# Streaming encoder layer on one core: 32 of 44 k-tiles of the down projection with the activations standing, the weights streaming 512 columns, and the sum turned by VectorE's block transposes

## The chip, the cores and the metric

The program runs on one core of a Trainium2 chip. The metric is the device time of one execution in microseconds (us), as the median of several runs. Beside the runs stands one profiled execution, whose rows are read below.

## What is computed

The reference is one layer of an encoder for 384 tokens (256 of a prompt, 8x16 of samples): two kinds of attention, then a gated feed-forward block, then an added embedding. All tensors are fp32. The change touches the third line alone:

```python
h = h + rms_norm(mix, g_post_mix)
f = rms_norm(h, g_pre_ffn)                                # (384, 2048)
f = (jax.nn.silu(f @ w_gate) * (f @ w_up)) @ w_down      # 2048 -> 5632 -> 2048
h = h + rms_norm(f, g_post_ffn)
return h + jax.nn.sigmoid(h @ w_ple_gate) * (p @ w_ple)
```

## The kernel before

Each fp32 matmul is done as three matmuls of a reduced fp32 type: weights and activations are split into a high part (ScalarE copies with a cast: `wh`, `sh`, `fh`) and a low part (VectorE subtracts: `wl`, `sl`, `fl`), and high x high, low x high and high x low are added up in a PSUM bank.

Weights come from memory in tiles of 128x2048 (`raw`, three buffers, loads issued by SyncE). `weights` cuts a tile into two half tiles of 128x1024 and `split` makes a `wh` and a `wl` of each. `wh` and `wl` have three buffers each, so a new half tile can be split when TensorE has done its last matmul with the one three before it.

The feed-forward block goes by eleven units of 512 hidden features. `gate_up(u)` computes a unit with the activations standing (the loaded operand is a 128x128 piece of `fh` or `fl`) and the weights streaming 512 columns: three banks, one for each 128 tokens, for the gate, three for the up part. ScalarE takes the gate from its banks through a Silu into `z` (128 tokens x 512 features, three times), VectorE multiplies the up part into it. `z` has tokens on the partitions. 16 block transposes of VectorE (blocks of 32x32, each instruction 32x384) turn it into `zT` with features on the partitions, and `to_hl` splits that into `sh` and `sl`, two 128-feature pieces to a buffer, five buffers.

The down projection works on groups of such pieces, `FGROUPS = (8, 8, 8, 8, 8, 4)`, 44 k-tiles in all. A group runs as soon as its pieces and one more are there: after units 2, 4, 6, 8 and 10, and the last of 4 right behind. For each of 16 tiles of 128 output features the weights stand and the activations stream 384 columns (`mm3`), into a bank `dn`. In the first group ScalarE copies the bank to `acc`, later VectorE adds it. The sum has output features on the partitions, as the norm and the residual behind it (`residual`) want it.

A scheduler fixes the order of instructions on each engine when the program is built, by priorities (`tc.high_priority`: weight splits are pulled ahead) and by its own estimate of times. On the chip an engine runs its instructions in that order. PSUM banks come from two sets of four: `dn` and the gate part use one, the up part the other.

Of the kernel before, what the change touches and what calls it, by code (L numbers as in the profile page):

```python
# [15 lines left out]
P = 128  # L16
# [40 lines left out]
def layer(ctx: ExitStack, tc: tile.TileContext, I, O):  # L57
# [76 lines left out]
    def g(col, n=0):  # L134
        return gains[:, col + n:col + n + 1]
# [686 lines left out]
    acc = ffn.tile([P, NK, T], F32, name="acc")  # L822

    def sq_add(ss, src, first, eng=dve):
        if first:
# [7 lines left out]
    for n in range(NK):  # L833
        ps = bank("mix")[:, :T]
        gemm(ps, weights(I["wout"][n]), mix, NK)
        act.copy(out=acc[:, n], in_=ps)
        sq_add(sm, acc[:, n], n == 0)

    def residual(ss, gcol, split_hl):

        low = []
        for n in range(NK):
            with ExitStack() as order:
                if n >= LEAD:
# [43 lines left out]
    residual(sm, G_POST, lambda n: scaled_hl(f(n), hh[:, n], g(G_FPRE, n)))  # L888
    rf = ffn.tile([P, 3], F32, name="rf")

    def by_token(out, w, k):

        for c in range(3):
            ah, al = f(k, slice(c * P, (c + 1) * P))
            pe.matmul(out[c], lhsT=ah, rhs=w[0], start=k == 0, stop=False)  # L895
            pe.matmul(out[c], lhsT=ah, rhs=w[1], start=False, stop=False)  # L896
            pe.matmul(out[c], lhsT=al, rhs=w[0], start=False, stop=k == NK - 1)  # L897

    def first_unit():

        gu = [[bank("gu", tag) for _ in range(3)] for tag in "gs"]
        for c in range(NK // 2):
            raw = stream.tile([P, 2048], F32, name="raw", tag="raw")
            with tc.high_priority(offset=PRIO):
                if c == 0:
                    subs = []
                    for i in range(2):
                        piece = raw[:, i * 1024:(i + 1) * 1024]
                        sp.dma_start(out=piece, in_=I["wgu0"][c][:, i * 1024:(i + 1) * 1024])
                        subs += split(piece, 1024)  # L910
                else:
                    sp.dma_start(out=raw, in_=I["wgu0"][c])
                    subs = split(raw, 2048)
            for i in range(2):
                for n in range(2):
                    by_token(gu[n], at(subs[i], slice(None), slice(n * 512, n * 512 + 512)), 2 * c + i)
        return gu

    gu0 = first_unit()
# [9 lines left out]
    def gate_up(u):  # L929
# [21 lines left out]
        zT = ffn.tile([P, 4, T], F32, name="zT", tag="zT")  # L951
        src = z.rearrange("p c (n f) -> p c n f", n=4)
        dst = zT.rearrange("p n (c t) -> p c n t", c=3)
        for j in range(4):
            for i in range(4):
                rows, cols = slice(32 * i, 32 * i + 32), slice(32 * j, 32 * j + 32)
                dve.transpose(out=dst[cols, :, :, rows], in_=src[rows, :, :, cols])  # L957
# [11 lines left out]
    for gi, gn in enumerate(FGROUPS):  # L969
        while len(ready) < gn + (1 if todo else 0) and todo:  # L970
            ready += gate_up(todo.pop(0))
        for n in range(NK):
            if n % 2 == 0:
                per = gn * P
# [5 lines left out]
            if gi == 0:  # L980
                act.copy(out=acc[:, n], in_=ps)
                continue
            with tc.high_priority(offset=2 * PRIO if gi == len(FGROUPS) - 1 else 0):
                dve.tensor_tensor(out=acc[:, n], in0=acc[:, n], in1=ps, op=ALU.add)  # L984
                if gi == len(FGROUPS) - 1:
                    sq_add(sd, acc[:, n], n == 0)
        ready = ready[gn:]


    embedding(1, sd)  # L990
    h2 = Pair("h2")
# [141 lines left out]
```

## Time and profile before

| | us |
|---|---|
| median of 3 runs | 1902.37 (1901.04 to 1902.71) |
| the profiled execution | 1902.81 |
| its span, first to last instruction | 1901.0 |
| TensorE busy in the span | 1883.6 |
| VectorE busy | 974.7 |
| ScalarE busy | 690.2 |

The span is what the rows of the profile lie in; the profiled execution's time is 1.8 us longer. A busy time counts an engine as busy while any of its instructions has a row that runs. Matmul rows overlap, so the pace of TensorE is read from the starts of its rows. The granted TensorE clock is 0.998 of full speed over the span.

### The profile page before, as it was taken

Reading aid. Unit: us, or ns where it says so; the run is one execution under the profiler, and the core shown is the slowest. Engines: PE = TensorE matmul, PEld = TensorE weight load, DVE = VectorE, ACT = ScalarE, POOL = GpSimd, SP = SyncE. Lnnn points to the kernel's source line nnn. Section 1 sums busy time; section 2 is a strip of 40 time slices with the busy share of each in tenths; the row PEclk is TensorE's granted clock in tenths of the full one; section 3 lists DMA queues with packets and bytes.
Section 4 is the critical chain, followed back from the end, with each engine's and each line's share of the span. In section 5 each row is a group of like instructions: output and inputs, shape, how many; then the busy total and the mean of one; then the engine's idle time right before and its main releaser. Section 6 shows DMA issues by size and latency. Waiting matters only on the chain.

```text
span 1901.0 us, 24107 instructions
## 1 busy us (share of the span) xinstructions
PE 1883.6 (99%) x10026; PEld 1709.8 (90%) x10026; DVE 974.7 (51%) x1368; ACT 690.2 (36%) x1044; POOL 80.4 (4%) x122
## 2 busy tenths in 40 slices
PE   8999999999999999999999999999999999999998
PEld 8989998788999988889988998899888988899998
DVE  7445756754233395445334643554355435456753
ACT  4344545643233453333333222322232222325432
POOL 4000002411000000000000000000000000000010
PEclk9999999999999999999999999999999999999999
DMA  6333325635743333343333333333333333334351
GB/s 239 136 110 112 112 89 176 213 138 204 258 169 133 130 122 133 111 136 130 133 133 123 122 133 133 129 118 130 133 133 111 133 133 133 111 111 147 128 177 67
DMA packets 43311, 262.53 MB, mean 138 GB/s; under 512 B 5441, under 2 KB 6481, under 8 KB 17090
## 3 DMA queue, kind: packets, MB, share of 16 engines
q1 hardware_dynamic: 36018, 233.76, 35.7%
q0 software_dynamic: 7184, 27.23, 4.1%
q8 instruction: 78, 1.28, 0.3%
q14 instruction: 31, 0.25, 0.0%
HBM read 251.17 MB, written 8.75 MB: 137 GB/s over the span
## 4 chain that ended last, share of the span: by engine, by line
PE 78%; DVE 1%; ACT 0%; issue 0%; DVEq 0%; ACTq 0%
PE gu L896 12%; PE gu L897 12%; PE gu L895 12%; PE dn L101 6%; PE dn L100 6%; PE dn L99 6%; PE mix L101 2%; PE pg L99 2%; PE pg L101 2%; PE pg L100 2%; PE mix L99 2%; PE mix L100 2%; PE psc L774 2%; PE pol L800 2%; PE ps L704 0%; DVE zT L957 0%
## 5 line engine op out<-in xcount | busy, mean ns | idle before, releaser
L90 DVE TENSOR_TENSOR wl<-raw,wh 128x1024 fp32r<-128x1024 f32 (+2 forms) x426 | 512.0, 1203 | 652.5 <-ACT wh L89 651.5
L89 ACT CAST wh<-raw 128x1024 fp32r<-128x1024 f32 (+2 forms) x426 | 435.8, 1023 | 980.5 <-PE gu L897 448.8
L896 PE MATMUL gu<-wl,fh 128*128 128x512 f32 x1056 | 411.5, 390 | 0.1
L897 PE MATMUL gu<-wh,fl 128*128 128x512 f32 x1056 | 409.2, 389 | 0.0
L895 PE MATMUL gu<-wh,fh 128*128 128x512 f32 x1056 | 406.9, 389 | 0.1
L896 PEld LDWEIGHTS gu<-wl,fh 128*128 128x128 f32 x1056 | 198.2, 188 | 42.7 <-DVE wl L90 1.7
L895 PEld LDWEIGHTS gu<-wh,fh 128*128 128x128 f32 x1056 | 198.2, 188 | 41.3 <-ACT fh L113 0.4
L897 PEld LDWEIGHTS gu<-wh,fl 128*128 128x128 f32 x1056 | 198.2, 188 | 41.0
L99 PE MATMUL dn<-sh,wh 128*128 128x384 f32 x704 | 235.1, 334 | 0.0
L100 PE MATMUL dn<-sl,wh 128*128 128x384 f32 x704 | 235.1, 334 | 0.0
L101 PE MATMUL dn<-sh,wl 128*128 128x384 f32 x704 | 234.7, 335 | 0.0
L101 PEld LDWEIGHTS dn<-sh,wl 128*128 128x128 f32 x704 | 132.0, 188 | 1.3 <-DVE wl L90 1.3
L99 PEld LDWEIGHTS dn<-sh,wh 128*128 128x128 f32 x704 | 132.1, 188 | 0.2
L100 PEld LDWEIGHTS dn<-sl,wh 128*128 128x128 f32 x704 | 132.1, 188 | 0.2
L957 DVE STREAM_TRANSPOSE zT<-z 32x384 f32<-32x384 f32 x176 | 100.3, 570 | 2.8
L984 DVE TENSOR_TENSOR acc<-acc,dn 128x384 f32<-128x384 f32 x80 | 44.3, 553 | 99.2 <-PE dn L101 98.8
L99 PE MATMUL mix<-mixh,wh 128*128 128x384 f32 x256 | 85.6, 334 | 0.0
L101 PE MATMUL pg<-h2h,wl 128*128 128x384 f32 x256 | 85.5, 334 | 0.0
L100 PE MATMUL pg<-h2l,wh 128*128 128x384 f32 x256 | 85.5, 334 | 0.0
L100 PE MATMUL mix<-mixl,wh 128*128 128x384 f32 x256 | 85.5, 334 | 0.0
L101 PE MATMUL mix<-mixh,wl 128*128 128x384 f32 x256 | 85.5, 334 | 0.0
L99 PE MATMUL pg<-h2h,wh 128*128 128x384 f32 x256 | 82.6, 334 | 0.0
(358 smaller groups left out, 2417.9 us busy)
## 6 DMA issues: line engine op xcount, KB each, us to landing
raw<-in_wgu SPq DMA_DIRECT2D x87, 1024.0 KB, 4.8
raw<-in_wd SPq DMA_DIRECT2D x40, 1024.0 KB, 4.8
raw<-in_win SPq DMA_DIRECT2D x20, 1024.0 KB, 4.9
raw<-in_wout SPq DMA_DIRECT2D x16, 1024.0 KB, 4.8
raw<-in_wpg SPq DMA_DIRECT2D x10, 1024.0 KB, 4.8
raw<-in_wvg SPq DMA_DIRECT2D x8, 1024.0 KB, 4.9
keys<-in_ckT POOLq DMA_DIRECT2D x8, 1024.0 KB, 5.6
raw<-in_ck SPq DMA_DIRECT2D x8, 1024.0 KB, 5.0
```

Of the source, the lines that this page charges most:

```text
L89: act.copy(out=h[:, :n], in_=raw[:, c:c + n])
L90: dve.tensor_tensor(out=l[:, :n], in0=raw[:, c:c + n], in1=h.bitcast(F32)[:, :n], op=ALU.subtract)
L99: pe.matmul(out, lhsT=w[0], rhs=a[0], start=start, stop=False)
L100: pe.matmul(out, lhsT=w[0], rhs=a[1], start=False, stop=False)
L101: pe.matmul(out, lhsT=w[1], rhs=a[0], start=False, stop=stop)
L774: pe.matmul(ps[:, :HK], lhsT=q.rearrange("p h t -> p (h t)"), rhs=keys[:, j, i * HK:(i + 1) * HK], start=j == 0, stop=j == 4)
L800: pe.matmul(o, lhsT=vals[:, k, j * P:(j + 1) * P], rhs=pT[:, k], start=k == 0, stop=False)
L895: pe.matmul(out[c], lhsT=ah, rhs=w[0], start=k == 0, stop=False)
L896: pe.matmul(out[c], lhsT=ah, rhs=w[1], start=False, stop=False)
L897: pe.matmul(out[c], lhsT=al, rhs=w[0], start=False, stop=k == NK - 1)
L957: dve.transpose(out=dst[cols, :, :, rows], in_=src[rows, :, :, cols])
L984: dve.tensor_tensor(out=acc[:, n], in0=acc[:, n], in1=ps, op=ALU.add)
```

## The change

The first four groups (`TOKG = 4`, 32 k-tiles) now run like the gate and up parts: `chunk_by_token` lets the activations stand and streams the weights in pieces of 512 output features, from a new arrangement of the same weights (`wdt`). One chunk is 512 output features: three banks for the three token blocks, 8 k-tiles, 72 matmuls of 512 columns; a group has four chunks. The sum of these groups, in four tiles `chunk0` to `chunk3` of 128x1536, has tokens on the partitions. After the fourth group `turn` transposes each chunk into features on the partitions with 16 block transposes, 64 in all, one chunk into a fifth tile and each next one into the place of the last. The last two groups (8 and 4 k-tiles) run as before and add to the turned sum. The fifth tile takes the place of `zT`, and later `chunk3`.

`chunk_by_token` also serves `gate_up`. It works the last quarter of a bank set bank by bank (all four k-tiles of one token block, then of the next) where the loop was by k-tile before.

```diff
+    chunks = [ffn.tile([P, 4 * T], F32, name=f"chunk{i}") for i in range(5)]
+    by_tok = [x.rearrange("p (c f) -> p c f", c=3) for x in chunks]
+    by_feat = [x.rearrange("p (n t) -> p n t", n=4) for x in chunks]
...
+    def turn(dst, src):
+
+        src = src.rearrange("p c (n f) -> p c n f", n=4)
+        dst = dst.rearrange("p n (c t) -> p c n t", c=3)
+        for j in range(4):
+            for i in range(4):
+                rows, cols = slice(32 * i, 32 * i + 32), slice(32 * j, 32 * j + 32)
+                dve.transpose(out=dst[cols, :, :, rows], in_=src[rows, :, :, cols])
...
+    def chunk_by_token(banks, srcs, a, nk):
+
+        for q, src in enumerate(srcs):
+            subs = weights(src)
+            order = [(k, c) for k in range(4) for c in range(3)]
+            if q == nk // 4 - 1:
+                order = [(k, c) for c in range(3) for k in range(4)]
+            for k, c in order:
+                kk = 4 * q + k
+                ah, al = a(kk, slice(c * P, (c + 1) * P))
+                w = at(subs[k // 2], slice(None), slice((k % 2) * 512, (k % 2) * 512 + 512))
+                by_token(banks[c], ah, al, w, kk == 0, kk == nk - 1)
...
-                for q in range(4):
-                    subs = weights(I["wgu"][8 * (u - 1) + 4 * i + q])
-                    for k in range(4):
-                        by_token(banks, at(subs[k // 2], slice(None), slice((k % 2) * 512, (k % 2) * 512 + 512)), 4 * q + k)
+                at_u = 8 * (u - 1) + 4 * i
+                chunk_by_token(banks, [I["wgu"][at_u + q] for q in range(4)], f, NK)
...
+        if gi < TOKG:
+            for n in range(4):
+                banks = [bank("dn") for _ in range(3)]
+                at_n = 8 * gi + 2 * n
+                chunk_by_token(banks, [I["wdt"][at_n + q] for q in range(2)],
+                               lambda k, t: (ready[k][0][:, t], ready[k][1][:, t]), 8)
+                for c in range(3):
+                    if gi == 0:
+                        act.copy(out=by_tok[n][:, c], in_=banks[c])
+                    else:
+                        dve.tensor_tensor(out=by_tok[n][:, c], in0=by_tok[n][:, c], in1=banks[c], op=ALU.add)
+            ready = ready[gn:]
+            if gi == TOKG - 1:
+
+                acc = []
+                for n in range(4):
+                    turn(by_feat[n - 1 if n else 4], by_tok[n])
+                    acc += [by_feat[n - 1 if n else 4][:, i] for i in range(4)]
+            continue
```

The order of VectorE's queue shows what moves. The first place is the border between the fourth group of the down projection and unit 9. Before, VectorE adds a bank (`acc`) and splits a half tile (`wl`) in turn, then splits for unit 9 (from `wl_10073` on):

```order
L984 TENSOR_TENSOR acc_4419<-acc_4419,dn_9932 128x384
L90 TENSOR_TENSOR wl_10027<-raw_10024,wh_10026 128x1024
L984 TENSOR_TENSOR acc_4419<-acc_4419,dn_9968 128x384
L90 TENSOR_TENSOR wl_10031<-raw_10024,wh_10030 128x1024
L109 TENSOR_TENSOR sl_9519<-zT_9495,sh_9518 128x384 x2
L984 TENSOR_TENSOR acc_4419<-acc_4419,dn_9994 128x384
L90 TENSOR_TENSOR wl_10073<-raw_10070,wh_10072 128x1024
L90 TENSOR_TENSOR wl_10077<-raw_10070,wh_10076 128x1024
L90 TENSOR_TENSOR wl_10119<-raw_10116,wh_10118 128x1024
L90 TENSOR_TENSOR wl_10123<-raw_10116,wh_10122 128x1024
```

Now the same place has the transposes of the sum (`chunk4` from `chunk0`, `chunk0` from `chunk1`) from the last chunk of the group on, here between the splits for that chunk (`wl_10873`) and the first of unit 9 (`wl_10986`, `wl_10990`):

```order
L110 TENSOR_TENSOR sl_10518<-chunk4_4423,sh_10517 128x384 x2
L836 STREAM_TRANSPOSE chunk4_4423<-chunk0_4419 32x3x4x32 x4
L91 TENSOR_TENSOR wl_10873<-raw_10866,wh_10872 128x1024
L836 STREAM_TRANSPOSE chunk4_4423<-chunk0_4419 32x3x4x32 x11
L91 TENSOR_TENSOR wl_10986<-raw_10983,wh_10985 128x1024
L836 STREAM_TRANSPOSE chunk4_4423<-chunk0_4419 32x3x4x32
L836 STREAM_TRANSPOSE chunk0_4419<-chunk1_4420 32x3x4x32 x6
L91 TENSOR_TENSOR wl_10990<-raw_10983,wh_10989 128x1024
L1002 TENSOR_TENSOR chunk3_4422<-chunk3_4422,dn_10817 128x512
L836 STREAM_TRANSPOSE chunk0_4419<-chunk1_4420 32x3x4x32
L1002 TENSOR_TENSOR chunk3_4422<-chunk3_4422,dn_10818 128x512
```

and goes on with the rest of them up to the seventh half tile of unit 9 (`wl_11124`):

```order
L836 STREAM_TRANSPOSE chunk0_4419<-chunk1_4420 32x3x4x32
L1002 TENSOR_TENSOR chunk3_4422<-chunk3_4422,dn_10819 128x512
L91 TENSOR_TENSOR wl_11032<-raw_11029,wh_11031 128x1024
L836 STREAM_TRANSPOSE chunk0_4419<-chunk1_4420 32x3x4x32 x8
L836 STREAM_TRANSPOSE chunk1_4420<-chunk2_4421 32x3x4x32 x14
L91 TENSOR_TENSOR wl_11036<-raw_11029,wh_11035 128x1024
L836 STREAM_TRANSPOSE chunk1_4420<-chunk2_4421 32x3x4x32 x2
L91 TENSOR_TENSOR wl_11078<-raw_11075,wh_11077 128x1024
L836 STREAM_TRANSPOSE chunk2_4421<-chunk3_4422 32x3x4x32 x7
L91 TENSOR_TENSOR wl_11082<-raw_11075,wh_11081 128x1024
L836 STREAM_TRANSPOSE chunk2_4421<-chunk3_4422 32x3x4x32 x9
L91 TENSOR_TENSOR wl_11124<-raw_11121,wh_11123 128x1024
```

Eight splits now stand between or behind 64 transposes; 22 of these are in a row, ahead of `wl_11036`. The first row, `sl_10518`, is the low part of unit 8's last pieces; it waits for a buffer that TensorE releases with the 26th matmul of the last chunk.

The second place is the end of a unit, here unit 5, with unit 6 behind it. Before, VectorE multiplies the three banks of the up part, transposes four times, splits the third half tile of the next unit, transposes twelve times and splits the fourth:

```order
L946 SCALAR_TENSOR_TENSOR z_8704<-gu_8895,rf_5606,z_8704 128x512
L946 SCALAR_TENSOR_TENSOR z_8704<-gu_8896,rf_5606,z_8704 128x512
L946 SCALAR_TENSOR_TENSOR z_8704<-gu_8897,rf_5606,z_8704 128x512
L957 STREAM_TRANSPOSE zT_9085<-z_8704 32x3x4x32 x4
L90 TENSOR_TENSOR wl_9167<-raw_9164,wh_9166 128x1024
L957 STREAM_TRANSPOSE zT_9085<-z_8704 32x3x4x32 x12
L90 TENSOR_TENSOR wl_9171<-raw_9164,wh_9170 128x1024
```

Now a split stands between the multiplications (`wl_8915`, the second half tile of the next unit), the third (`wl_8957`) behind them, and the 16 transposes are in one block ahead of the fourth (`wl_8961`):

```order
L91 TENSOR_TENSOR wl_8911<-raw_8908,wh_8910 128x1024
L971 SCALAR_TENSOR_TENSOR z_8495<-gu_8686,rf_5610,z_8495 128x512
L971 SCALAR_TENSOR_TENSOR z_8495<-gu_8687,rf_5610,z_8495 128x512
L91 TENSOR_TENSOR wl_8915<-raw_8908,wh_8914 128x1024
L971 SCALAR_TENSOR_TENSOR z_8495<-gu_8688,rf_5610,z_8495 128x512
L91 TENSOR_TENSOR wl_8957<-raw_8954,wh_8956 128x1024
L836 STREAM_TRANSPOSE chunk4_4423<-z_8495 32x3x4x32 x16
L91 TENSOR_TENSOR wl_8961<-raw_8954,wh_8960 128x1024
```

The split of the second half tile has moved behind two of the multiplications, and four transposes have moved behind the third split. At unit ends with a down group behind them the order of VectorE's rows is the same.

## Rows read from the trace of the kernel before

**Rows 1.** The page, busy us (share of the span) and instructions of each engine.

```profile
PE 1883.6 (99%) x10026; PEld 1709.8 (90%) x10026; DVE 974.7 (51%) x1368; ACT 690.2 (36%) x1044; POOL 80.4 (4%) x122
```

**Rows 2.** The page, chain that ended last: shares by engine, by line.

```profile
PE 78%; DVE 1%; ACT 0%; issue 0%; DVEq 0%; ACTq 0%
PE gu L896 12%; PE gu L897 12%; PE gu L895 12%; PE dn L101 6%; PE dn L100 6%; PE dn L99 6%; PE mix L101 2%; PE pg L99 2%; PE pg L101 2%; PE pg L100 2%; PE mix L99 2%; PE mix L100 2%; PE psc L774 2%; PE pol L800 2%; PE ps L704 0%; DVE zT L957 0%
```

**Rows 3.** Timeline of TensorE: start us, length us, engine, line, what it computes.

```profile
699.73 0.39 PE L896 MATMUL gu<-wl,fh 128*128 128x512 f32 x1
...
711.74 0.39 PE L895 MATMUL gu<-wh,fh 128*128 128x512 f32 x1
...
1499.71 0.33 PE L99 MATMUL dn<-sh,wh 128*128 128x384 f32 x1
...
1516.18 0.33 PE L101 MATMUL dn<-sh,wl 128*128 128x384 f32 x1
```

**Rows 4.** The page, costliest groups: out<-in xcount, busy us, mean ns, idle before.

```profile
L90 DVE TENSOR_TENSOR wl<-raw,wh 128x1024 fp32r<-128x1024 f32 (+2 forms) x426 | 512.0, 1203 | 652.5 <-ACT wh L89 651.5
L89 ACT CAST wh<-raw 128x1024 fp32r<-128x1024 f32 (+2 forms) x426 | 435.8, 1023 | 980.5 <-PE gu L897 448.8
...
L957 DVE STREAM_TRANSPOSE zT<-z 32x384 f32<-32x384 f32 x176 | 100.3, 570 | 2.8
L984 DVE TENSOR_TENSOR acc<-acc,dn 128x384 f32<-128x384 f32 x80 | 44.3, 553 | 99.2 <-PE dn L101 98.8
```

**Rows 5.** Timeline of VectorE at the end of a unit before a down group.

```profile
1059.40 2.11 DVE L946 SCALAR_TENSOR_TENSOR z<-gu,rf,z 128x512 f32<-128x512 f32 x3 [0.41 <-PE gu L897]
1061.54 2.31 DVE L957 STREAM_TRANSPOSE zT<-z 32x384 f32<-32x384 f32 x4
1063.88 1.23 DVE L90 TENSOR_TENSOR wl<-raw,wh 128x1024 fp32r<-128x1024 f32 x1
1065.14 7.00 DVE L957 STREAM_TRANSPOSE zT<-z 32x384 f32<-32x384 f32 x12
1072.17 0.56 DVE L984 TENSOR_TENSOR acc<-acc,dn 128x384 f32<-128x384 f32 x1
1072.65 1.22 DVE L90 TENSOR_TENSOR wl<-raw,wh 128x1024 fp32r<-128x1024 f32 x1
```

**Rows 6.** Timeline of TensorE in the same stretch.

```profile
1073.58 0.34 PE L100 MATMUL dn<-sl,wh 128*128 128x384 f32 x1
1073.92 0.44 PE L101 MATMUL dn<-sh,wl 128*128 128x384 f32 x1
1074.20 0.34 PE L99 MATMUL dn<-sh,wh 128*128 128x384 f32 x1
```

**Rows 7.** Waits of weight loads: engine, line, for whom, us in total, times, longest us.

```profile
PEld gu L896 <- DVE wl L90: 1.7, 6, 0.6
...
PEld dn L101 <- DVE wl L90: 1.3, 4, 0.3
```

**Rows 8.** Windows behind a wait: us, busy PE, PEld, DVE, ACT, POOL, PEclk, DMA, GB/s.

```profile
38.00:39.00 1.00, 1.00 (x5) 0.56 (x3) 1.00 (x2) 0.00 (x0) 0.00 (x0) 0.65 0.00 0
39.00:40.00 1.00, 0.73 (x3) 0.66 (x3) 1.00 (x3) 0.00 (x0) 0.00 (x0) 0.50 0.00 0
40.00:41.00 1.00, 1.00 (x4) 0.80 (x3) 0.49 (x1) 0.00 (x0) 0.00 (x0) 0.50 0.69 106
41.00:42.00 1.00, 1.00 (x4) 0.60 (x3) 0.00 (x0) 0.07 (x1) 0.00 (x0) 0.64 0.87 344
42.00:43.00 1.00, 1.00 (x8) 1.00 (x7) 0.00 (x0) 0.97 (x2) 0.00 (x0) 1.00 0.97 410
```

**Rows 9.** Timeline of TensorE in the same microseconds.

```profile
37.11 0.44 PE L101 MATMUL qg<-ah,wl 128*128 128x384 f32 x1 [2.34 <-DVE wl L90]
...
39.83 0.52 PE L99 MATMUL qg<-ah,wh 128*128 128x384 f32 x1
40.15 0.52 PE L100 MATMUL qg<-al,wh 128*128 128x384 f32 x1
```

More of the change, by code (lines that the diff above doesn't have):

```diff
@@ L35 @@
 FGROUPS = (8, 8, 8, 8, 8, 4)
+TOKG = 4
 WIDE = 6
@@ L821, in layer, with by_token @@
     pool.dma_start(out=hh, in_=I["xT"])
-    acc = ffn.tile([P, NK, T], F32, name="acc")
+    chunks = [ffn.tile([P, 4 * T], F32, name=f"chunk{i}") for i in range(5)]
+    by_tok = [x.rearrange("p (c f) -> p c f", c=3) for x in chunks]
+    by_feat = [x.rearrange("p (n t) -> p n t", n=4) for x in chunks]
+    acc = [by_feat[n // 4][:, n % 4] for n in range(NK)]
+    def turn(dst, src):
[5 more added lines that the diff above has]
+                dve.transpose(out=dst[cols, :, :, rows], in_=src[rows, :, :, cols])
+    def by_token(out, ah, al, w, start, stop):
+        pe.matmul(out, lhsT=ah, rhs=w[0], start=start, stop=False)
+        pe.matmul(out, lhsT=ah, rhs=w[1], start=False, stop=False)
+        pe.matmul(out, lhsT=al, rhs=w[0], start=False, stop=stop)
+    def chunk_by_token(banks, srcs, a, nk):
[9 more added lines that the diff above has]
+                by_token(banks[c], ah, al, w, kk == 0, kk == nk - 1)
     def sq_add(ss, src, first, eng=dve):
@@ L835, in layer, with residual @@
         gemm(ps, weights(I["wout"][n]), mix, NK)
-        act.copy(out=acc[:, n], in_=ps)
-        sq_add(sm, acc[:, n], n == 0)
-    def residual(ss, gcol, split_hl):
+        act.copy(out=acc[n], in_=ps)
+        sq_add(sm, acc[n], n == 0)
+    def residual(acc, ss, gcol, split_hl):
         low = []
@@ L887, in layer @@
     sf = [sf[:, n, :T] for n in range(2)]
-    residual(sm, G_POST, lambda n: scaled_hl(f(n), hh[:, n], g(G_FPRE, n)))
+    residual(acc, sm, G_POST, lambda n: scaled_hl(f(n), hh[:, n], g(G_FPRE, n)))
     rf = ffn.tile([P, 3], F32, name="rf")
[L891 to L897, printed above, removed]
     def first_unit():
@@ L915, in first_unit @@
                 for n in range(2):
-                    by_token(gu[n], at(subs[i], slice(None), slice(n * 512, n * 512 + 512)), 2 * c + i)
+                    k, w = 2 * c + i, at(subs[i], slice(None), slice(n * 512, n * 512 + 512))
+                    for t in range(3):
+                        by_token(gu[n][t], *f(k, slice(t * P, (t + 1) * P)), w, k == 0, k == NK - 1)
         return gu
@@ L950, in gate_up @@
                     act.preload_act_table_set("natural_log_exp_and_others")
[L951 to L957, printed above, removed]
+        zT = by_feat[4 if u < 2 * TOKG + 1 else 3]
+        turn(zT, z)
         out = []
@@ L979, in layer @@
                 mm3(ps, at(w, slice(None), slice(k * P, (k + 1) * P)), ready[k], k == 0, k == gn - 1)
-            if gi == 0:
-                act.copy(out=acc[:, n], in_=ps)
-                continue
             with tc.high_priority(offset=2 * PRIO if gi == len(FGROUPS) - 1 else 0):
-                dve.tensor_tensor(out=acc[:, n], in0=acc[:, n], in1=ps, op=ALU.add)
+                dve.tensor_tensor(out=acc[n], in0=acc[n], in1=ps, op=ALU.add)
                 if gi == len(FGROUPS) - 1:
-                    sq_add(sd, acc[:, n], n == 0)
+                    sq_add(sd, acc[n], n == 0)
         ready = ready[gn:]
@@ L991, in layer @@
     h2 = Pair("h2")
-    residual(sd, G_FPOST, lambda n: to_hl(h2(n), hh[:, n]))
+    residual(acc, sd, G_FPOST, lambda n: to_hl(h2(n), hh[:, n]))
     first = gemm_wide(I["wpg0"], h2, "pg")
@@ L1105 @@
     at = 0
+    wdt = x["w_down"][0][:8 * TOKG * P].reshape(TOKG, 2, 4, P, 4, 512).transpose(0, 4, 1, 3, 2, 5)
+    arrays["wdt"] = wdt.reshape(8 * TOKG, P, 2048)
     for i, n in enumerate(FGROUPS):
-        arrays[f"wd{i}"] = _packed(x["w_down"][0][at * P:(at + n) * P], 2)
+        if i >= TOKG:
+            arrays[f"wd{i}"] = _packed(x["w_down"][0][at * P:(at + n) * P], 2)
         at += n
```

2 lines of the change are left out of this document (1 added, 1 removed).

## Prediction

> **What bounds the kernel now.** The page's engine list came first: TensorE is busy 1883.6 of 1901.0 us and VectorE half of it [rows 1], and the chain that ended last is TensorE for 78% of the span, with every large link a gate/up or down matmul [rows 2]. So the pace of TensorE and its rare waits set the time. "Busy" must not be read as the pace. A matmul's row lasts 0.33 us (384 columns) or 0.39 us (512 columns), but the rows overlap; what counts is the distance of their starts. 96 down matmuls in a row start from 1499.71 to 1516.18 us, 95 steps of 0.1734 us; 54 gate/up matmuls start from 699.73 to 711.74 us, 53 steps of 0.2266 us [rows 3]. Counted by half tiles of weights (128x1024, high and low part) that is 18 x 0.2266 = 4.08 us each in gate/up and 24 x 0.1734 = 4.16 us each in the down projection.
>
> The second thing to see is who feeds TensorE. Each half tile is cast by ScalarE (1.02 us) and split by VectorE (1.20 us on average) [rows 4]; there are three buffers for each part, so at most two half tiles, some 8 us, lie ready ahead of TensorE. VectorE waits most of the time, but its rows come in the order of its program, so a split that stands behind other work is late by that work. At the end of a unit it has 16 block transposes to do, and there it is nearly late already [rows 5]: three multiplications to 1061.51 us, 4 transposes, a split, 12 transposes in 7.00 us (0.583 us each), a sum, and a split that ends at 1073.87 us. TensorE needs that one: its matmul starts at 1073.92, 0.34 us behind its neighbour, not 0.17, and the next step is 0.28 [rows 6]. It lost 0.28 us. All waits of weight loads in gate/up and down for VectorE's low part are 1.7 and 1.3 us [rows 7].
>
> **What it removes.** 32 of the 44 k-tiles change form. Before, 32x16x3 = 1536 matmuls of 384 columns at 0.1734 us: 266.3 us. Now 32x4x3x3 = 1152 of 512 columns at 0.2266 us: 261.0 us. The same sum by half tiles: 64 of them, each 4.08 instead of 4.16 us, gives 5.1 us. I take **-5.2 us**. The columns streamed are the same 589,824; what goes is the fixed part of 384 matmuls. From the two steps that is 0.2266 - 512 x (0.2266 - 0.1734)/128 = 0.0138 us each [rows 3], and 384 of them are 5.3 us. The Trainium skill (TensorE: Matmul & The Clock Gate, section "Wait — 56ns, not 53.3ns?") gives a fixed cost of about 2.5 ns for each matmul behind its columns; by that, an estimate, only 1.0 us would go. The measured steps here differ from it and decide.
>
> **What stays equal.** Weights arrive in the same number of 1 MB tiles and are split in the same 128x1024 pieces. 12 copies of 128x512 by ScalarE replace 16 of 128x384, and 36 sums of 128x512 by VectorE replace 48 of 128x384. No row shows such a sum; the nearest, three 128x512 multiplications from a bank in 2.11 us, give 0.70 us [rows 5], so 25 us for 48 x 0.55 = 27 us [rows 4]. They lie beside matmuls, and a chunk's banks leave slack: of four banks each chunk takes three, so its first bank is free, and in the last quarter, worked bank by bank, the chunk before is done with its first bank 5.4 us before its end. The longest delay of a sum is three multiplications and splits, some 3 us, and the next chunk's third bank is asked for about 4 us after release. I take 0; if the slack is gone, a microsecond at each of 15 chunk borders.
>
> **What it adds, first: the turn.** After the fourth group 64 transposes turn the sum from token to feature order. Each has the shape of those in the units (32x384, three blocks of four), so 64 x 0.583 = 37.3 us of VectorE [rows 5]. Nothing on TensorE needs their result for two units, some 130 us. But the order of VectorE's queue, shown above, puts only eight splits between them. I follow it from t = 0, the start of the group's last chunk of 72 matmuls. The low part of the last activations, which stands ahead of the transposes, waits for a buffer that TensorE releases with the chunk's 26th matmul: t = 5.9; a cast and two VectorE rows later, 0.5 us each by the sums of the same 128x384 [rows 4], t = 7.5, the transposes start. Up to the split of the seventh half tile of the next unit VectorE has
>
> - 64 transposes, 37.3 us,
> - 8 splits at 1.26 us from start to start, 10.1 us [rows 5],
> - 3 sums at 0.70 us, 2.1 us,
>
> 49.5 us in all; it ends at t = 57.0. TensorE without a wait would ask for that half tile after 72 + 6x18 + 3 = 183 matmuls, 41.5 us (three need only the high part). It starts 0.1 us after the split, as in [rows 5, 6]: **+15.6 us**. By the same count the loss falls in four pieces: before the first split of the unit 2.4 us, the second 4.0, the fourth 7.3 (22 transposes stand ahead of that one) and the seventh 2.0. The bounds: were the cover complete, 0; were VectorE to work alone, all 37.3 us. Because the terms are all rows of the same engine and shape, I stay near the middle value, 13 to 18 us.
>
> **Second: the unit ends.** Gate/up now works its last quarter bank by bank. That holds the buffer of a half tile until 6 matmuls before the end T of the unit, 1.4 us, not 18 matmuls. The split of the second half tile behind T so ends at T + 1.0 us (cast and split, 1.02 + 1.23 us after release [rows 4, 5]), where it ended before T; the last multiplication ends at T + 1.7, the third split at T + 2.95, and the 16 transposes stand in one block now, 9.3 us, to T + 12.3. The fourth split ends at T + 13.5 us. By the order of TensorE's queue it asks for it after 57 matmuls where gate/up follows (T + 12.9, 0.6 us lost, five times), after 58 where a down group follows (T + 13.1, 0.45 us lost, four times), and after 76 of 384 columns in the fifth group, with a sum ahead of the split (T + 13.2 against T + 14.1, 0.9 us lost). That is 5.7 us, where the same ends lose some 1.6 us now [rows 6, 7]: **+4.1 us**. The losses are differences of sums of a dozen terms, so each may be 0.3 us off: 1 to 7 us.
>
> **The sum.** The profiled execution took 1902.8 us (span 1901.0), 0.4 us over the median of the runs. 1902.8 - 5.2 + 15.6 + 4.1 = 1917.3; less the 0.4, **1917 us**, 0.8% slower.
>
> **Rivals.** A, my forecast: VectorE's queue at the turn costs more than the steps save.
>
> B, the other side: the turn is hidden, as VectorE's idle half suggests, and the 5.2 us come through less the unit ends: 1902.4 - 5.2 + 1 = 1898 us at best. For it speaks that VectorE waits 651 us for ScalarE's casts [rows 4], and that nobody waits for the turned sum. Against it: the cover on TensorE is 8 us of ready weights, not 130 us, because the splits stand behind the transposes. It decides below 0.34 us a transpose, where 64 of them no longer make TensorE wait; the 176 of the trace take 0.57 each [rows 4].
>
> C, hardly a change: turn and unit ends cost about what the steps save, 1899 to 1906 us. With 4.1 us at the unit ends it needs a turn of 5 us or less, a third of what the rows of one engine add up to.
>
> D, the clock: a fall of TensorE's clock behind the stall adds to it. Once in mid-kernel the trace shows one. A wait of 2.34 us for VectorE ends at 37.11 us [rows 9]; the granted clock (the seventh number) is 0.65 in the 39th microsecond, 0.50 in the next two, 0.64 in the 42nd and 1.00 again from 42 us [rows 8], and matmuls of 384 columns start 0.32 us apart, which is 1.2 GHz, where 0.173 us is 2.4 GHz [rows 9]. The lost work is 0.35 + 0.50 + 0.50 + 0.36 = 1.7 us. The Trainium skill (TensorE: Matmul & The Clock Gate, section "The HAM clock gate") has an idle TensorE throttled to half until it has been busy again; by that rule, and these rows agree, the clock falls in the turn too. But there most of it is swallowed: behind the pieces of 2.4 and 4.0 us stands a longer wait, and behind that of 7.3 us the 2.0 us before the seventh split. Only a fall behind the last piece, or a second one, is paid: 1.7 us each, 1919 to 1921 us.
>
> **Chances.** A 0.58, D 0.33, C 0.06, B 0.03; A is the likeliest and gives the time. A alone spans 1911 to 1922 at its farthest (turn 13 to 18, unit ends 1 to 7), and its two terms hardly meet at one end. With D the upper end is 1923; 3 us below A's corner leave room for a smaller turn: 1908 to 1923. 0.2%, 3.8 us, is about what a measurement tells from no change, so B is faster and C the same: faster 0.03, same 0.06, slower 0.91.
>
> **What would show it.** Right: down steps of 0.2266 us; a new wait of weight loads for VectorE's low part, some 15 us, in the first 40 us of the unit behind the fourth group, with the longest near 7 us; and 0.4 to 0.6 us at unit ends. Transposes near 0.57 us, 240 of them. Granted clock below 1 in that stretch would show D. Wrong would make it: transposes between sums that are faster than those in the units, a TensorE that has more weights ready than I count at t = 0, or a wait at the chunk borders for a bank.

## The result, and the profile of the changed kernel

The changed kernel takes 1914.55 us (median of 4 runs, 1913.94 to 1916.71) where the kernel before, run beside it, takes 1902.54 us: a ratio of 1.0065 with a 95% interval of [1.005, 1.008]. Run again later it took 1917.52 us beside 1901.18 us, 1.0084 [1.007, 1.0098]. The forecast was 1917 us. The profiled execution took 1914.81 us, its span is 1913.0 us.

The page's engine list and its chain that ended last, to be read against [rows 1, 2]:

```profile
PE 1883.5 (98%) x9642; PEld 1660.1 (87%) x9642; DVE 1003.2 (52%) x1420; ACT 690.4 (36%) x1040; POOL 80.3 (4%) x122
...
PE 68%; DVE 10%; issue 1%; ACT 1%; DVEq 0%
```

TensorE has 384 instructions less and the same busy time, VectorE 28.5 us more, where the 64 transposes take 36.4. Busy times say nothing of the 12 us. The chain points to them: VectorE's share of it went from 1% to 10%, so there are stretches now in which the end hangs on VectorE's rows, one behind the other.

The waits say where. Engine, line, for whom, us in total, times, longest:

```profile
PEld gu L841 <- DVE wl L91: 17.1, 10, 5.8
...
PE gu L841 <- DVE wl L91: 12.5, 9, 5.4
```

The wait for the low part of a weight split was 1.7 us in gate/up [rows 7] and is 17.1 us now, most of it in a few long pieces. They lie in the turn. VectorE there (L836 are the transposes of the sum, L91 the splits, L1002 the sums of the last chunk):

```profile
1507.64 1.03 DVE L110 TENSOR_TENSOR sl<-chunk,sh 128x384 fp32r<-128x384 f32 x2 [3.90 <-ACT sh L109]
1508.70 2.33 DVE L836 STREAM_TRANSPOSE chunk<-chunk 32x384 f32<-32x384 f32 x4
1511.06 1.23 DVE L91 TENSOR_TENSOR wl<-raw,wh 128x1024 fp32r<-128x1024 f32 x1
1512.32 6.51 DVE L836 STREAM_TRANSPOSE chunk<-chunk 32x384 f32<-32x384 f32 x11
1518.86 1.23 DVE L91 TENSOR_TENSOR wl<-raw,wh 128x1024 fp32r<-128x1024 f32 x1
1520.12 4.13 DVE L836 STREAM_TRANSPOSE chunk<-chunk 32x384 f32<-32x384 f32 x7
1524.28 1.23 DVE L91 TENSOR_TENSOR wl<-raw,wh 128x1024 fp32r<-128x1024 f32 x1
...
1529.91 13.01 DVE L836 STREAM_TRANSPOSE chunk<-chunk 32x384 f32<-32x384 f32 x22
1542.95 1.22 DVE L91 TENSOR_TENSOR wl<-raw,wh 128x1024 fp32r<-128x1024 f32 x1
...
1557.18 3.50 DVE L91 TENSOR_TENSOR wl<-raw,wh 128x1024 fp32r<-128x1024 f32 x3
```

And TensorE, from the start of the group's last chunk:

```profile
1501.22 0.39 PE L840 MATMUL dn<-wh,sh 128*128 128x512 f32 x1
...
1520.14 0.79 PE L841 MATMUL gu<-wl,fh 128*128 128x512 f32 x1 [2.21 <-DVE wl L91]
1520.73 0.63 PE L842 MATMUL gu<-wh,fl 128*128 128x512 f32 x1
1521.16 0.63 PE L840 MATMUL gu<-wh,fh 128*128 128x512 f32 x1
...
1525.56 0.50 PE L841 MATMUL gu<-wl,fh 128*128 128x512 f32 x1 [2.49 <-DVE wl L91]
...
1544.23 0.79 PE L841 MATMUL gu<-wl,fh 128*128 128x512 f32 x1 [5.43 <-DVE wl L91]
...
1558.46 0.50 PE L841 MATMUL gu<-wl,fh 128*128 128x512 f32 x1 [0.34 <-DVE wl L91]
```

Each wait ends 0.05 us behind the end of a split, which VectorE does as soon as it is through the transposes ahead of it: 1518.86 + 1.23 = 1520.09 and TensorE starts at 1520.14; 1525.51 and 1525.56; 1544.17 and 1544.23. From the chunk's first matmul to the one that needs the seventh half tile of unit 9 it is 1558.46 - 1501.22 = 57.24 us, against 183 steps of 0.2266 us, 41.5 us, without a wait. 15.8 us are lost in this stretch, when the distances of all starts beyond 0.2266 us are added up.

The clock falls in it three times. Windows of two us; the seventh number is the granted clock:

```profile
1518.00:1520.00 2.00, 0.00 (x0) 0.00 (x0) 1.94 (x3) 1.01 (x1) 0.00 (x0) 0.98 0.00 0
1520.00:1522.00 2.00, 1.86 (x4) 1.49 (x5) 1.89 (x5) 0.00 (x0) 0.00 (x0) 0.50 0.00 0
1522.00:1524.00 2.00, 1.06 (x3) 0.33 (x1) 1.92 (x4) 0.00 (x0) 0.00 (x0) 0.67 0.00 0
1524.00:1526.00 2.00, 0.44 (x2) 0.40 (x3) 1.97 (x3) 0.00 (x0) 0.00 (x0) 1.00 0.00 0
...
1528.00:1530.00 2.00, 2.00 (x6) 1.52 (x6) 1.94 (x4) 0.00 (x0) 0.00 (x0) 0.50 0.80 336
...
1544.00:1546.00 2.00, 1.77 (x4) 1.49 (x5) 1.91 (x4) 0.00 (x0) 0.00 (x0) 0.50 0.38 78
```

At 0.50, which is 1.2 GHz, the matmuls start 0.43 us apart (1521.16 - 1520.73), where it is 0.2266 at 2.4 GHz. The 15.8 us hold these slow steps as well as the waits.

The end of a unit, here with a down group behind it, to be read against [rows 5, 6]: VectorE, then TensorE.

```profile
1057.65 1.23 DVE L91 TENSOR_TENSOR wl<-raw,wh 128x1024 fp32r<-128x1024 f32 x1 [1.70 <-ACT wh L90]
1058.80 0.74 DVE L971 SCALAR_TENSOR_TENSOR z<-gu,rf,z 128x512 f32<-128x512 f32 x1
1059.46 1.22 DVE L91 TENSOR_TENSOR wl<-raw,wh 128x1024 fp32r<-128x1024 f32 x1
1060.59 9.31 DVE L836 STREAM_TRANSPOSE chunk<-z 32x384 f32<-32x384 f32 x16
1069.92 2.36 DVE L91 TENSOR_TENSOR wl<-raw,wh 128x1024 fp32r<-128x1024 f32 x2
```

```profile
1070.42 0.61 PE L840 MATMUL dn<-wh,sh 128*128 128x512 f32 x2
1071.20 0.50 PE L841 MATMUL dn<-wl,sh 128*128 128x512 f32 x1 [0.17 <-DVE wl L91]
```

The 16 transposes are one block of 9.31 us now, and the split behind it ends at 1071.15 us. Two steps of 0.2266 us behind 1070.42, at 1070.87, TensorE would have started its third matmul; it starts at 1071.20, and with a longer step behind that 0.44 us are lost. Such ends lost 0.67 us before a gate/up unit (five), 0.44 or 0.45 before a down group (four), 0.81 before the fifth group.

Stage by stage, each from the start of its first matmul to that of the next stage's first:

| | before | after |
|---|---|---|
| first down group | 863.27 to 929.85: 66.58 | 860.71 to 926.47: 65.76 |
| second and third | 66.88, 66.88 | 65.76, 65.76 |
| two units between | 130.70, 130.68, 130.73 | 131.25, 131.28, 131.28 |
| fourth group, units 9 and 10 | 1455.72 to 1653.28: 197.56 | 1451.80 to 1664.74: 212.94 |
| first gate/up matmul to the end of the span | 665.36 to 1901.0: 1235.6 | 662.19 to 1913.0: 1250.8 |

### The profile page after: what moved, and what is told of

Same layout as the page of the kernel before. It is cut to its first block, busy times and chain, and to the rows that moved or that the text cites. A ratio compares the mean times of both kernels' runs of the same rounds, so it can differ in the third digit from the quotient of the medians.

```text
span 1913.0 us, 23382 instructions
## 1 busy us (share of the span) xinstructions
PE 1883.5 (98%) x9642; PEld 1660.1 (87%) x9642; DVE 1003.2 (52%) x1420; ACT 690.4 (36%) x1040; POOL 80.3 (4%) x122
## 3 DMA queue, kind: packets, MB, share of 16 engines
q8 instruction: 75, 1.23, 0.3%
## 4 chain that ended last, share of the span: by engine, by line
PE 68%; DVE 10%; issue 1%; ACT 1%; DVEq 0%
PE gu L841 11%; PE gu L842 11%; PE gu L840 10%; DVE chunk L836 7%; PE dn L841 4%; PE dn L842 3%; PE dn L840 3%; PE pg L102 2%; PE pg L100 2%; PE mix L101 2%; PE mix L102 2%; PE mix L100 2%; PE pg L101 2%; DVE wl L91 2%; PE psc L775 2%; PE dn L102 2%
## 5 line engine op out<-in xcount | busy, mean ns | idle before, releaser
L91 DVE TENSOR_TENSOR wl<-raw,wh 128x1024 fp32r<-128x1024 f32 (+2 forms) x426 | 507.7, 1194 | 660.0 <-ACT wh L90 657.3
L841 PE MATMUL gu<-wl,fh 128*128 128x512 f32 x1056 | 410.8, 392 | 12.6 <-DVE wl L91 12.5
L840 PE MATMUL gu<-wh,fh 128*128 128x512 f32 x1056 | 397.1, 391 | 0.1
L841 PEld LDWEIGHTS gu<-wl,fh 128*128 128x128 f32 x1056 | 199.4, 189 | 58.2 <-DVE wl L91 17.1
L841 PE MATMUL dn<-wl,sh 128*128 128x512 f32 x384 | 149.7, 390 | 0.7 <-DVE wl L91 0.7
L842 PE MATMUL dn<-wh,sl 128*128 128x512 f32 x384 | 148.3, 389 | 0.0
L840 PE MATMUL dn<-wh,sh 128*128 128x512 f32 x384 | 141.9, 389 | 0.0
L836 DVE STREAM_TRANSPOSE chunk<-z 32x384 f32<-32x384 f32 x176 | 100.2, 569 | 2.3
L841 PEld LDWEIGHTS dn<-wl,sh 128*128 128x128 f32 x384 | 72.1, 188 | 17.2 <-DVE wl L91 2.4
L840 PEld LDWEIGHTS dn<-wh,sh 128*128 128x128 f32 x384 | 72.1, 188 | 15.0
L842 PEld LDWEIGHTS dn<-wh,sl 128*128 128x128 f32 x384 | 72.1, 188 | 14.9
L1043 POOL DMA_DIRECT2D out_yT<-tmp x14 | 7.6, 543 | 1402.1 <-DVE tmp L1042 1398.1
```

The lines of the kernel that those rows point to most:

```text
L91: dve.tensor_tensor(out=l[:, :n], in0=raw[:, c:c + n], in1=h.bitcast(F32)[:, :n], op=ALU.subtract)
L840: pe.matmul(out, lhsT=ah, rhs=w[0], start=start, stop=False)
L841: pe.matmul(out, lhsT=ah, rhs=w[1], start=False, stop=False)
L842: pe.matmul(out, lhsT=al, rhs=w[0], start=False, stop=stop)
L1043: (pool if n < NK - 2 else sp).dma_start(out=O["yT"][n * P:(n + 1) * P, sl], in_=z[:, sl])
```

## The experiments

Beside each run's time stands its ratio to the kernel before, run on the same chip in turn with it: 1902.54 us for the changed kernel, 1901.24 for the next four rows, 1901.18 for "after again" and the last row, 1900.81 for the others. The last column is worked out as in the last line of the table above, from the run's own trace; it leaves out what happens ahead of the feed-forward block.

| | median us | ratio [95%] | first gate/up matmul to end, us |
|---|---|---|---|
| before | 1901.24 (27 runs), 1900.81 (16), 1901.18 (9) | | 1235.6 |
| after | 1914.55 | 1.0065 [1.005, 1.008] | 1250.8 |
| turn left out | 1900.59 | 0.9997 [0.9988, 1.0006] | 1235.1 |
| turn spread | 1900.36 | 0.9997 [0.9988, 1.0006] | 1235.0 |
| old order in gate/up | 1910.78 | 1.0048 [1.0035, 1.0061] | 1245.4 |
| before, bank by bank | 1906.40 | 1.0024 [1.0015, 1.0033] | 1241.3 |
| turn twice | 1927.07 | 1.0138 [1.0124, 1.0152] | 1261.0 |
| after again | 1917.52 | 1.0084 [1.007, 1.0098] | 1252.0 |
| turn spread, old order | 1895.09 | 0.9968 [0.9957, 0.998] | 1229.4 |
| all transposes spread | 1892.17 | 0.9958 [0.9945, 0.9971] | 1228.5 |
| before, `mixl` on VectorE | 1898.70 | 0.9988 [0.9979, 0.9997] | 1235.3 |
| all spread, `mixl` on VectorE | 1890.76 | 0.9947 [0.9933, 0.996] | 1228.0 |

The theory throughout, called Q in the expectations, is the forecast's: a split of weights is late by the work that VectorE's program puts ahead of it.

**The turn left out.**

```diff
-        zT = by_feat[4 if u < 2 * TOKG + 1 else 3]
+        zT = by_feat[4]
...
-                    turn(by_feat[n - 1 if n else 4], by_tok[n])
-                    acc += [by_feat[n - 1 if n else 4][:, i] for i in range(4)]
+                    acc += [by_feat[n][:, i] for i in range(4)]
```

> The changed kernel without the 64 transposes of the sum; what the last two groups add to and the residual reads is then the sum in the wrong layout, so this part of the computation is left out. Theory Q (VectorE's queue at the turn holds back the weight splits): the turn's 15.8 us go, 1914.6 - 15.8 = about 1899 us, a little faster than before. Rival C (the chunk form itself loses: waits for banks, slower matmuls, later sums): the time stays within 3 us of 1914.6. Rival D (the falls of TensorE's clock carry the loss): between the two, the pure wait of 11 us goes and some 5 us stay only if the clock also falls elsewhere; without a long wait it should not fall, so D predicts the same as Q here but through the clock, and a profile without any fall in the unit behind the fourth group.

It took 1900.59 us, 14.0 us less than the changed kernel, and the stretch from the first gate/up matmul on is 15.7 us shorter. The time is no lower than that of the kernel before: the 5.2 us saved and the losses at the unit ends nearly cancel. The 1.6 us above the 1899 expected lie ahead of the block, which begins at 663.71 us in this profile and at 662.19 in that of the changed kernel. In the trace nothing is lost behind the fourth group, the clock does not fall there, and the unit ends lose what they lose in the changed kernel. So the turn costs 15 to 16 us and nothing else in the change costs as much. This does not say yet whether it is the transposes or their place.

**The turn spread.** The same 64 transposes, four behind each of unit 9's 16 splits:

```diff
-                    turn(by_feat[n - 1 if n else 4], by_tok[n])
+                    waiting.extend(turn_steps(by_feat[n - 1 if n else 4], by_tok[n]))
...
+    def drain(per=4):
+        for low in low_parts[-2:]:
+            with tc.issue_after(low.ins):
+                for _ in range(min(per, len(waiting))):
+                    o, s = waiting.pop(0)
+                    dve.transpose(out=o, in_=s)
```

> All of the computation is kept: the 64 transposes of the sum are done during unit 9, four behind each of its 16 weight splits, in place of all at once. Theory Q: VectorE has 4.08 us for a half tile, of which a split takes 1.26 and four transposes 2.33 us, so TensorE never waits for them: about 1899 us as without the turn. Rival W (the transposes themselves cost TensorE time wherever they lie, for example by a slower weight cast or matmul beside them): 1905 to 1914 us. Rival C: within 3 us of 1914.6.

1900.36 us, as without the turn; from the first gate/up matmul on it is 1235.0 us against 1235.1. Rival W is out. VectorE in the same place of this kernel:

```profile
1524.77 1.23 DVE L93 TENSOR_TENSOR wl<-raw,wh 128x1024 fp32r<-128x1024 f32 x1 [1.73 <-ACT wh L92]
1526.02 2.38 DVE L853 STREAM_TRANSPOSE chunk<-chunk 32x384 f32<-32x384 f32 x4
1528.44 1.23 DVE L93 TENSOR_TENSOR wl<-raw,wh 128x1024 fp32r<-128x1024 f32 x1
1529.58 2.35 DVE L853 STREAM_TRANSPOSE chunk<-chunk 32x384 f32<-32x384 f32 x4
1531.96 1.23 DVE L93 TENSOR_TENSOR wl<-raw,wh 128x1024 fp32r<-128x1024 f32 x1
```

A split and four transposes take 3.6 us, less than the 4.08 us of matmuls that a half tile feeds. The work is all there and no matmul waits for it. So the loss came from the place in the queue.

**The turn twice.** Each chunk's 16 transposes done a second time into the same place:

```diff
-                    turn(by_feat[n - 1 if n else 4], by_tok[n])
+                    for _ in range(2):
+                        turn(by_feat[n - 1 if n else 4], by_tok[n])
```

> The changed kernel with each chunk's 16 transposes done twice into the same place, so 128 transposes in the turn; the result is the same. Theory Q (VectorE's queue: a split of weights is late by the transposes, splits and sums that the program puts ahead of it): the order of VectorE's queue now spreads them over 17 splits, and the split that decides is the 16th half tile of unit 9, with 123 transposes, 17 splits and 3 sums ahead: 7.5 + 71.7 + 21.4 + 2.1 = 102.7 us behind the start of the group's last chunk, where TensorE without waits would ask for it after 345 matmuls, 78.2 us: 24.5 us lost in the turn against 15.8 measured in the changed kernel, so about 1914.6 + 9 = 1923.5 us. Rival P (a transpose has a price of its own on TensorE's path, 15.8/64 = 0.25 us each, wherever it stands): 31.6 us lost, 1930 us. Rival X (the loss is a fixed disturbance of the border between group and unit): unchanged, 1914.6 us.

1927.07 us, so by its median it lies between the two: Q's 1923.5 is just below the interval (1.0124 of 1900.8 is 1924.4), P's 1930 just above (1929.7). The trace separates them. The turn lost 25.5 us in it, added up as above, against Q's 24.5 and P's 31.6. 16.7 of them are lost by 1551 us, where blocks of up to 22 transposes stand ahead of a split, as in the changed kernel. The other 8.8 us come in nine pieces of 0.2 to 1.9 us, where five to eight transposes stand between splits: eight and a split are 6.0 us, more than the 4.08 us of a half tile, five are 4.2. So a transpose has no price of its own; what counts is the sum between two splits. From the first gate/up matmul on it is 10.2 us longer than the changed kernel. Its median is 12.5 us longer. Of the 2.3 us between, the two profiles show 1.0 ahead of the block (it begins at 663.19 us, against 662.19); the rest lies between executions, which the next run was for.

**The changed kernel again**, beside the kernel before.

> The changed kernel again, unaltered, beside the kernel before on the same chip, to place the doubled turn: that run lost 25.5 us in the turn by its trace, 9.7 us more than the changed kernel, but its median stood 12.5 us above it, with the runs before it on another chip. Theory Q (the turn's cost is what the trace shows as waits, 15.8 us, and the rest of that difference comes from the part of the kernel ahead of the feed-forward block, which varies from execution to execution): a turn loss of 15.8 us again, and a time of 1914 to 1918 us, with a start of the feed-forward block between 661 and 666 us. Rival (the doubled transposes cost more than the waits show): 1914.5 us or less, with the same start as before.

1917.52 us, with 16.7 us lost in the turn, and the feed-forward block began at 663.95 us, not 662.19. The doubled turn is then 9.6 us above it, where Q has 9. Its four times are 1913.9 and 1917.4 to 1917.9 us, the first four were 1913.9 to 1914.8 and 1916.7: two clusters some 3 us apart. Of the 2.9 us between the two profiled executions, one of each cluster, 1.8 lie ahead of the block, where the section "Ahead of the feed-forward block" looks, and 1.1 in it, nearly all in the turn.

**The order of gate/up's last quarter**, put back in the changed kernel, and put alone into the kernel before:

```diff
-            if q == nk // 4 - 1:
+            if q == 1 and nk == 8:
```

> The changed kernel, but gate/up works its last quarter k-tile by k-tile as before; only the down chunks work theirs bank by bank. Theory Q with unit ends: TensorE loses 0.1 to 0.3 us at each unit end in place of 0.44 to 0.82, so 3 to 5 us less than 1914.6: 1910 to 1911.5 us. Rival: if the order of the last quarter does not matter, 1914.6 within 1 us.

```diff
-                    for k in range(4):
-                        by_token(banks, at(subs[k // 2], ...), 4 * q + k)
+                    order = [(k, c) for k in range(4) for c in range(3)]
+                    if q == 3:
+                        order = [(k, c) for c in range(3) for k in range(4)]
+                    for k, c in order:
+                        by_token(banks, at(subs[k // 2], ...), 4 * q + k, (c,))
```

> The kernel before, with one part of the change alone: gate/up works its last quarter bank by bank. Theory Q with unit ends: 0.56 us lost at five ends in place of about 0.2, a little more at the ends before down groups and 0.5 at the fifth group: 3 to 4.5 us over 1902.5, so 1905.5 to 1907 us. Rival: within 1 us of 1902.5.

Put back, 1910.78 us, 5.4 us less from the first gate/up matmul on; the ends lose 0.08 us before a gate/up unit, nothing before the first four down groups and 0.26 before the fifth, and the turn still 15.8 us. Alone in the kernel before, 1906.40 us: inside the 1905.5 to 1907 expected, but these were reckoned from 1902.5 us. Over the 1901.24 us beside it, it is 5.2 us more, and 5.7 from the first gate/up matmul on, where 3 to 4.5 were expected. That was a miss in size: the ends lose 0.67 us before a gate/up unit, where 0.56 was expected, and 0.80 before the second to the fifth down group (0.38 before the first). There the old down projection has a sum of 0.55 us ahead of the late split:

```profile
1062.95 9.30 DVE L960 STREAM_TRANSPOSE zT<-z 32x384 f32<-32x384 f32 x16
1072.29 0.55 DVE L987 TENSOR_TENSOR acc<-acc,dn 128x384 f32<-128x384 f32 x1
1072.76 1.22 DVE L90 TENSOR_TENSOR wl<-raw,wh 128x1024 fp32r<-128x1024 f32 x1
```

**Both costs out.** The spread turn with the old order in gate/up:

> The changed kernel with both costs taken out: the transposes of the sum four behind each of unit 9's splits, and gate/up's last quarter k-tile by k-tile as before the change (the new down chunks keep the order bank by bank). Theory Q: what stays is the saving of the steps, 5.2 us, and unit ends that lose 0.1 to 0.3 us each as before, some 0.6 us less in all: 1901.2 - 5.2 - 0.6 = 1895.4 us, ratio 0.997. Rival (the steps' saving is not real on the whole kernel, and the two runs at 1900.5 had it from elsewhere): 1900 us, no difference to the kernel before.

1895.09 us, ratio 0.9968 [0.9957, 0.998]: faster than the kernel before, by 5.7 us where 5.8 were expected. A down group of 72 x 4 matmuls takes 65.28 us in it, each of the four, against 66.58 for a group before that loses nothing: 1.30 us, and four times that is 5.2 us. The saving of the steps was there all along.

**All transposes spread.** On top of that the units' own 16 transposes, and the low parts behind them, two behind each split of what follows:

```diff
-        turn(zT, z)
+        waiting.extend(turn_steps(zT, z))
...
+            drain(4 if len(waiting) > 24 else 2)
...
-            to_hl(out[-1], zT[:, n])
+            waiting.append((out[-1], zT[:, n], dve))
```

> As the run with both costs taken out, and the 16 transposes and the four low parts of each unit's activations (units 0 to 9) spread as well, two behind each split of the next half unit or chunk, instead of in one block at the unit's end. Theory Q: no split is late at these unit ends, so nothing is lost there: 0.1 to 0.5 us below the run with both costs out, some 1895 us. Rival (the spread rows delay splits at the borders of chunks, where sums stand among them, or the low part behind the group's last chunk holds VectorE up): a loss at each of some ten ends, 1897 us or more.

1892.17 us, 0.9958 [0.9945, 0.9971], faster than both kernels. Nothing is lost at unit ends (0.40 us at the first unit's before), but for the last, ahead of the fifth group, which was left as it was: 0.27 us. From the first gate/up matmul on it is 0.9 us shorter than the run before it. The rest of the 2.9 us between their medians, and so most of the miss against the 1895 expected, lies ahead of that by the two profiles: the block begins at 661.44 us in this one and at 664.68 in that of the run before it. The intervals overlap.

**Ahead of the feed-forward block.** The profile after had reached its first gate/up matmul 3.2 us earlier than the profile before, with the same instructions in the same order. Most of that is one split: of the 3.2 us, 2.6 come at 346 us, behind it, and the rest is the balance of smaller differences of both signs. VectorE and GpSimd in the kernel before:

```profile
338.12 7.48 DVE L90 TENSOR_TENSOR wl<-raw,wh 128x1024 fp32r<-128x1024 f32 x1
...
338.30 2.41 POOL L109 TENSOR_TENSOR mixl<-og,mixh 128x1024 fp32r<-128x1024 f32 x1
...
342.11 2.40 POOL L109 TENSOR_TENSOR mixl<-og,mixh 128x1024 fp32r<-128x1024 f32 x1
```

and in the changed kernel:

```profile
337.64 3.67 DVE L91 TENSOR_TENSOR wl<-raw,wh 128x1024 fp32r<-128x1024 f32 x1
...
337.81 2.41 POOL L110 TENSOR_TENSOR mixl<-og,mixh 128x1024 fp32r<-128x1024 f32 x1
...
341.63 2.41 POOL L110 TENSOR_TENSOR mixl<-og,mixh 128x1024 fp32r<-128x1024 f32 x1
```

A split of this shape takes 1.2 us. Here it ended 1.1 us behind the end of a GpSimd subtraction: the second in the execution before, the first in that after. Behind the split of 7.48 us TensorE waited 2.37 us for a VectorE row, in the changed kernel there is no such wait:

```profile
346.44 0.66 PE L574 MATMUL pk<-base,tmp 128*128 128x128 f32 x4 [2.37 <-DVE s L615]
```

It is not the change that decides which of the two it is. Of the ten profiles with GpSimd's subtractions, the split takes 7.48 us in seven, the second one of the changed kernel among them, and the block begins at 663.2 to 665.4 us; it takes 3.67 or 3.68 us in three, and the block begins at 660.8 to 662.2. The kernel before with both subtractions on VectorE:

```diff
-        to_hl(mix(slice(0, 8), sl), og[:, :, :, sl]..., pool if c < 2 else dve)
+        to_hl(mix(slice(0, 8), sl), og[:, :, :, sl]..., dve)
```

> The kernel before with two subtractions of 128x1024 (mixl, far ahead of the feed-forward block) on VectorE where GpSimd did them, 2.4 us each. In the profile before one weight split beside them took 7.48 us, in the profile after 3.67 us, and 1.21 us elsewhere. Theory V (a VectorE split that meets a GpSimd subtraction stands still until it is done): the long split goes, splits there take 1.2 us, and the feed-forward block begins some 2 to 5 us earlier than in the profile before: 1897 to 1900 us. Rival (the long split was hidden, or the two subtractions, 2.4 us more of VectorE, cost as much): 1901 us.

1898.70 us, 0.9988 [0.9979, 0.9997], and in its trace:

```profile
337.94 1.22 DVE L90 TENSOR_TENSOR wl<-raw,wh 128x1024 fp32r<-128x1024 f32 x1
339.07 1.22 DVE L109 TENSOR_TENSOR mixl<-og,mixh 128x1024 fp32r<-128x1024 f32 x1
```

The long split is gone and the block begins at 661.72 us, as in the profiles with the shorter of the two long splits. This bears theory V out: the subtractions take 1.22 us each on VectorE, 2.4 on GpSimd, where VectorE's split stood still beside them. How much of the 2.1 us between the medians is the split alone is not shown, since TensorE's matmuls come in another order in this kernel from 344 us on. Together with the spread transposes:

> The run with all transposes spread, and the two subtractions of mixl on VectorE as well. If the two gains add up: 1892.2 - 2.1 = 1890.1 us, a ratio of 0.9945 to the kernel before, no weight split over 1.5 us long around 337 us, and nothing lost at unit ends. Rival (the executions of the spread run had the shorter of the two long splits, 3.67 us, more often, and its time already holds the gain): 1892 us.

1890.76 us, 0.9947 [0.9933, 0.996], 0.5% below the kernel before, with its five times from 1890.1 to 1891.2 us. Its interval and that of the run with the transposes spread alone overlap, so that the two gains add up is likely and not shown.

## Why the prediction was right, step by step

**The steps, -5.2 us.** Right: four groups at 65.28 instead of 66.58 us, 5.2 us, in the run with the turn spread and the old order. The Trainium skill (TensorE: Matmul & The Clock Gate, section "Wait — 56ns, not 53.3ns?") has 2.5 ns for each matmul; by that, an estimate, it would have been 1.0 us. The trace has 13.6 ns for each of 384 matmuls and decides.

**What stays equal, 0.** Right: the first group takes 65.76 us in the changed kernel, 65.28 and a unit end of 0.45, so nothing is lost at its chunk borders. A sum of 128x512 takes 0.68 us, where 0.70 was read from the nearest row.

**The turn, +15.6 us.** 15.8 us in the first profile, 16.7 in the second, 15.8 with the old order. The count of VectorE's rows from the last chunk's start to the seventh half tile, 57.1 us, came out as 57.24. The four pieces are where they were put, but are split up otherwise: counted as distances of starts beyond one step, the waits are 2.4, 2.9, 5.6 and 0.5 us, where 2.4, 4.0, 7.3 and 2.0 were forecast, and the other 4.5 us are longer steps, nearly all of them at the lower clock (1.2, 1.7 and 1.5 us behind the first three waits). That is what the forecast had for rival D: the clock falls three times, and each fall is swallowed by the wait behind it, since VectorE, whose rows show no change of pace, sets when the last wait ends.

The second profile shows the same with other falls. Its clock, then the seventh split of unit 9 on VectorE (the first of the two in its row), and the matmul that needs it:

```profile
1522.00:1524.00 2.00, 1.67 (x6) 1.05 (x6) 1.89 (x5) 0.00 (x0) 0.00 (x0) 1.00 0.00 0
...
1546.00:1548.00 2.00, 1.77 (x4) 1.48 (x5) 1.91 (x4) 0.00 (x0) 0.00 (x0) 0.50 0.48 74
1548.00:1550.00 2.00, 2.00 (x6) 1.52 (x6) 1.97 (x4) 0.00 (x0) 0.00 (x0) 0.50 0.95 393
1550.00:1552.00 2.00, 2.00 (x7) 1.52 (x6) 1.96 (x4) 0.00 (x0) 0.00 (x0) 0.50 0.14 57
```

```profile
1559.19 2.36 DVE L91 TENSOR_TENSOR wl<-raw,wh 128x1024 fp32r<-128x1024 f32 x2
...
1561.45 0.39 PE L841 MATMUL gu<-wl,fh 128*128 128x512 f32 x1
```

Behind the first wait, to 1522.13 us, the clock does not fall. The second wait is 3.9 us, near the 4.0 of the forecast, and ends at 1527.55 us, 24.33 us behind the chunk's first matmul at 1503.22; in the first profile, with the fall, it ends 24.34 us behind it. So that fall cost nothing. Behind the third wait the clock stays at 0.50 for longer, the steps lose 3.0 us, and no wait is left before the seventh half tile. Its split ends at 1560.41 us, TensorE asks for it at 1561.45, 58.23 us behind the chunk's first matmul instead of 57.24 (which it is again with the old order). So 1.0 us of this fall was paid: a part of rival D's price, in one of these three profiles.

**The unit ends, +4.1 us.** Mechanism and size right: 5.9 us after, 1.5 before, so some 4.5. The run with the old order gives 5.4 us back from the first gate/up matmul on, nearly the whole of what they lose.

**The sum.** From the first gate/up matmul to the end: forecast -5.2 + 15.6 + 4.1 = 14.5 us, measured 15.2 and 16.3 us. The whole kernel's 12.0 and 16.3 us hold besides what lies ahead of the block, which no term had: the forecast's base, the profile before, had the longer split, the first profile after the shorter, and its 12 us are 15.2 less 3.2 that the change did not bring. That 1917 us lies so near to 1917.52, and 2.5 us from 1914.55, is therefore in part luck; the forecast's terms are tested by the 14.5 us against 15.2 and 16.3.

**The rivals.** B, the turn hidden, is out for this order of the queue, and is what happens with another (turn spread). C is out by the intervals. D's falls came; in the first profile its time did not, in the second 1.0 us of it did.

## What to carry to other kernels

Ask of an engine that idles half its time not how much work it has left over, but what stands ahead of the next instruction that the bound engine waits for; two half tiles of cover, some 8 us, were all that TensorE had here, and 64 transposes cost 15.8 us in blocks of up to 22 and nothing in fours. Work that nobody needs soon belongs between the splits, tied to them one by one; left to itself, the scheduler here put up to 22 transposes ahead of one split. Before a loss is given to a change, compare the stages that it does not touch: the 12 us between two profiles were 15.2 us lost in the block and 3.2 gained ahead of it, most of them a wait far upstream that comes and goes from execution to execution.

## What was unexpected of the hardware

A VectorE subtraction with both inputs in SBUF stood still for as long as a GpSimd subtraction ran that had started 0.17 us behind it, and in seven of ten profiles through a second one too, 1.4 us later: 3.67 and 7.48 us instead of 1.2. In the executions with 3.67 us the second subtraction met another VectorE row with two inputs (128x384, 1.65 or 1.66 us instead of 0.55). The Trainium skill (SBUF — State Buffer, section "Who interferes with whom") says that a VectorE instruction with two SBUF inputs contends with a GpSimd instruction that reads SBUF. The runs agree; that the one that is issued second is blocked, as the Trainium skill has it there, is not what the rows show, where the split starts first, but spans of GpSimd are rough. That VectorE would also wait in the 1.4 us between the two is not explained by any run here.

The clock was at half at 1520 and 1544 us as TensorE resumed behind waits of 2.2 and 5.4 us, but behind the wait of 2.49 us that ended at 1525.56 it first ran at 2.4 GHz, with steps of 0.23 us, and fell at 1526.8 us, when TensorE was busy again. In the second profile the same first wait of 2.2 us brought no fall at all. Why the fall comes at once in one place, late in another and not at all in a third was not tried.
